# A transformer layer on one core: GpSimd's block arithmetic on VectorE, and a quadrant of W_out read from its own tiles

## The chip, the core and the metric

The kernel runs on one core of a Trainium2 chip. The core has a matrix engine (TensorE, PE in the profile; its weight loads are PEld), a vector engine (VectorE, DVE), an engine for activations, casts and copies (ScalarE, ACT), a general engine (GpSimd, POOL) and SyncE (SP), whose queue issues most of the transfers. Each engine runs its own queue in order and waits for semaphores of the others. The metric is the device time of one execution in microseconds (us), lower is better.

## The reference

One layer of a bidirectional encoder for 1024 tokens of width 1024, all in float32:

```python
h = swiglu(rms_norm(x, g1a), ffn1_w_in, ffn1_w_out)      # (silu(x Wg) * (x Wu)) W_out, d_ff = 2816
x = x + 0.5 * rms_norm(h, g1b)
u = rms_norm(x, gma)
rq, rk, rv, rg, nq, nk, nv, g_ret, g_na = split(u @ w_mix_in)
y_ret = (silu(rg) * headnorm(retention(rotary(rq), rotary(rk), rv))) @ w_ret_out   # 4 heads, both directions
y_na  = neighbourhood_attention_2d(nq, nk, nv, rel_bias) @ w_na_out                # 8 heads, window 8 x 16
x = x + rms_norm((sigmoid(g_ret) * y_ret + sigmoid(g_na) * y_na) @ w_mix_out, gmb)
h = swiglu(rms_norm(x, g2a), ffn2_w_in, ffn2_w_out)
out = x + 0.5 * rms_norm(h, g2b)
```

## The kernel before

**Matmuls in three passes.** Each float32 operand is split in two parts for the matrix engine: `split` (line 56) has ScalarE cast the source to a rounded high half h (line 61), and another engine subtract it from the source to get the low half l (line 62). `mm3` (lines 88 to 90) multiplies high by high, high by low and low by high into one PSUM bank. Weights come by `raw` (a DMA on SP's queue into one of three `wraw` buffers of 128 x 1024), and `piece` splits half of one into tiles `wh` and `wl`, of which there are seven each.

**Winograd products.** The large projections are 2 x 2 block products in seven products in place of eight. `Winograd` (line 234) holds the seven left operands (a11, a12, a22, s1 to s4, each as h and l). `put` makes them from the transposed normed activations for each of eight token tiles: tiles 0 to 3 give a11 and a12, tiles 4 to 7 give a22 and the four sums, with lines 277 and 278 (s3), 283 and 285 (s1, s2), 288 and 289 (s4), and the splits of each. `put` returns the split of s4 as a function that the caller runs later. `Pairs` (line 316) is the loop over pairs of weight tiles: `run` loads two raw tiles g and u, makes the right-hand sums t1 to t4 on DVE (lines 380, 381, 389, 398), splits each and runs seven products of 12 matmuls; the results are added out of PSUM on DVE (lines 387 to 403). `lead` runs the first two products of some pairs ahead; six such pairs stand at the start of the kernel, three of them saved to SBUF by ScalarE.

**The first FFN.** The eight token tiles are normed (`norm_T`: ScalarE squares, GpSimd's `rstd` in line 98, DVE in line 118), transposed by TensorE (line 127) and put. Then `fin.lead` and `ffn_in`: 22 turns of `Pairs.run`, each with a SiLU on ScalarE (line 418) and the product with the up half on DVE (line 420). `LeftFactors` turns each two results into the seven left operands of the output projection: four sums on GpSimd (line 446), then seven splits (ScalarE in line 454, DVE in line 455), one after each product, stored to DRAM by DMAs on GpSimd's queue (line 68).

**ffn_out** multiplies these by W_out, with seven products of 11 k steps and 12 matmuls for each k. The operands g of a step come back from DRAM through `Blocks`, by SP's queue, and the right-hand operand is split by `piece`. The four quadrants of W_out are loaded in three transfers each into `tiles[i][j][n]` (n counts groups of four k). The first product, a11, reads quadrant (0,0): for k below 4 from raw buffers loaded on their own (`b11`), for others from its tiles. The same tiles are loaded whole, since the second product s1 needs t1(k) = (0,1) - (0,0), written over (0,0). `t1` to `t4` (through `sub`, line 559, with a fixed order among themselves) run on GpSimd at set steps. Each product ends with a pass over PSUM on DVE and ScalarE; `ep.square` (line 504) multiplies by the gain on GpSimd, and lines 593 and 594 are two more sums on it. Then norm, residual (line 514) and store.

**Mixing.** Fourteen jobs of `Pairs.run` make the projections; four of them (`fn == "rotary"`) end with `rotate` (lines 886 to 889, four instructions) for each of four parts, parts 0 and 2 on GpSimd and parts 1 and 3 on DVE. Then come neighbourhood attention, retention, gates, and `out_proj`, whose epilogue `Ep` adds the residual in line 229.

**Order.** A scheduler fixes the instructions of each engine at build time from priorities and dependences; the engines then follow that order. A waiting instruction holds up all that stands behind it on its engine.

Of the kernel before, what the change touches and what calls it, by code (L numbers as in the profile page):

```python
# [18 lines left out]
P = 128  # L19
# [19 lines left out]
class Core:  # L39
# [13 lines left out]
        nc.gpsimd.memset(self.mhalf, -0.5)  # L53
        self.small = None

    def split(self, h, l, src, scale=None, eng=None):

        nc = self.nc
        hf = h.bitcast(F32)
        if scale is None:  # L60
            nc.scalar.copy(h, src)  # L61
            (eng or nc.vector).tensor_tensor(l, src, hf, ALU.subtract)  # L62
# [9 lines left out]
        self.nc.sync.dma_start(raw[:, :n], src)  # L72
        return raw

    def piece(self, src, eng=None):
# [3 lines left out]
        self.split(h, l, src, eng=eng)  # L79
        return h, l  # L80

    def load_w(self, src):
# [116 lines left out]
class Ep:  # L199
# [12 lines left out]
    def __call__(self, t, banks):  # L212
        c, nc = self.c, self.c.nc
        y = self.pool.tile([P, D], F32, tag="tmp", name="tmp", bufs=3)
        x = self.pool.tile([P, D], F32, tag="epx", name="epx", bufs=2)
        nc.sync.dma_start(x, self.resid(t))
        ss = c.small.tile([P, 3], F32, tag="ss3", name="ss3", bufs=6)
        f = 4.0 if self.half else 1.0
        for b in range(2):
            nc.scalar.activation(y[:, b * 512:(b + 1) * 512], banks[b], AF.Square,  # L220
                                 scale=(1.0 / 16.0 if self.half else 1.0 / 32.0), accum_out=ss[:, b:b + 1])
        nc.vector.tensor_scalar(ss[:, 2:3], ss[:, 0:1], ss[:, 1:2], f * EPS, ALU.add, ALU.add)
        r = c.rstd(ss[:, 2:3], 1)
        sx = c.small.tile([P, 3], F32, tag="ss3", name="ss3", bufs=6)
        for b in range(2):
            bs = slice(b * 512, (b + 1) * 512)
            nc.vector.scalar_tensor_tensor(y[:, bs], banks[b], r[:, 0:1], self.post[:, bs],
                                           op0=ALU.mult, op1=ALU.mult)
            (nc.gpsimd if t > 5 else nc.vector).tensor_tensor(x[:, bs], y[:, bs], x[:, bs], ALU.add)
            if self.pre is not None:  # L230
                nc.scalar.activation(y[:, bs], x[:, bs], AF.Square, scale=1.0 / 32.0, accum_out=sx[:, b:b + 1])
        (nc.sync.dma_start if self.pre is None else c.store)(self.dst(t), x)
        if self.pre is not None:
            return c.norm_T(x, self.pre, t, self.pool, self.put, sx)


class Winograd:
# [5 lines left out]

    def __init__(self, c, pools, tmp, bufs, spill=None):

        self.c, self.tmp, self.spill, self.s3_on_pool = c, tmp, spill, ()
# [11 lines left out]
    def put(self, t, g, pt):  # L258
        c, nc = self.c, self.c.nc
        ts = slice((t % 4) * P, (t % 4 + 1) * P)  # L260
        if t < 4:
            c.split(*self.part(("a11", "a12")[g], ts), pt)
            return

        def tmp():
            return self.tmp.tile([P, 4, P], F32, tag="cmb", name="cmb", bufs=4)

        h1, l1 = [q.bitcast(F32) for q in self.part("a11", ts)]
        h2, l2 = [q.bitcast(F32) for q in self.part("a12", ts)]

        if g == 0:
            self.a21, self.s3 = tmp(), tmp()
            nc.scalar.copy(self.a21, pt)
            if self.spill is not None:
                c.store(self.spill[:, :, ts], self.a21)
            eng = nc.gpsimd if t in self.s3_on_pool else nc.vector
            eng.tensor_tensor(self.s3, h1, self.a21, ALU.subtract)
            eng.tensor_tensor(self.s3, self.s3, l1, ALU.add)
# [9 lines left out]
        nc.gpsimd.tensor_tensor(s3, h2, s3, ALU.subtract)  # L288
        nc.gpsimd.tensor_tensor(s3, s3, l2, ALU.add)  # L289
        return lambda: c.split(*self.part("s4", ts), s3, eng=nc.gpsimd)  # L290


def xslice(xop):
# [6 lines left out]
class Pairs:  # L300
# [6 lines left out]
        self.last = None  # L307
        self.between = lambda: None

    def product(self, a, b, eng=None):  # L310
        bank = self.c.bank()
        ah, al = self.x.op(a)
        b = self.c.piece(b, eng)
        for k in range(4):
            self.c.mm3(bank, [p[:, k * P:(k + 1) * P] for p in b], (ah[:, k], al[:, k]), k == 0, k == 3)
        self.between()
        return bank
# [12 lines left out]
                               k == 0, k == 3)  # L330
                    yield

    def lead(self, save=None, between=(), on_pool=()):

        n = self.held + self.saved
        for i in (*range(self.held, n), *range(self.held)):
            if i in self.begun:
                continue
            g = self.c.raw(self.srcs[i][0])
            eng = self.c.nc.gpsimd if i in on_pool else None  # L340
            ps = [self.product("a11", g[:, :512], eng), self.product("a12", g[:, 512:], eng)]
            if between:
                f = between.pop(0)()
                if f is not None:
# [81 lines left out]
class LeftFactors:  # L426
# [6 lines left out]
        self.c, self.tmp, self.parts, self.dst, self.later = c, tmp, parts, dst, []  # L433

    def __call__(self, i, gt):
        c, eng, j = self.c, self.c.nc.gpsimd, i // 2
        if i % 2 == 0:
            self.a11, self.a21 = gt[:, 512:], gt[:, :512]
            return
# [44 lines left out]
class Epilogue:  # L484
# [12 lines left out]
            if g is not None:  # L497
                self.c.nc.sync.dma_start(g, src)

    def square(self, t, b, h, junk, out=None, eng=None):  # L500

        c = self.c
        c.nc.scalar.activation(junk, h, AF.Square, scale=1.0 / 16.0, accum_out=self.ss[t][0][:, b:b + 1])
        (eng or c.nc.gpsimd).tensor_tensor(h if out is None else out, h, self.post[:, b * 512:(b + 1) * 512], ALU.mult)

    def steps(self, t, x, halves):
        c, nc = self.c, self.c.nc
# [21 lines left out]
def ffn_out(c, tiles, q, blocks, w_out, gl, ep, side={}):  # L529
# [1 line left out]

    nc = c.nc
    NK = FT // 2
    tt, add = nc.vector.tensor_tensor, nc.gpsimd.tensor_tensor
    spare = [t[2][:, 3] for b in tiles for t in b]
    later, rest, flips, xs = [], [], [], {}

# [18 lines left out]
    order = []  # L556

    def sub(out, a, b):
        e = nc.gpsimd.tensor_tensor(out, a, b, ALU.subtract).ins  # L559
# [28 lines left out]
    def p7(u, b):  # L588
        tt(q[3][:, u], b, q[1][:, u], ALU.add)

        def more():
            xload(u)
            add(q[1][:, u], q[1][:, u], q[2][:, u], ALU.add)
            add(q[2][:, u], q[3][:, u], q[2][:, u], ALU.add)
            ep.square(u, 1, q[2][:, u], spare[u])
        later.extend((more, None))

# [16 lines left out]
    def p3(u, b):  # L614
        e = tt(q[1][:, u], b, q[1][:, u], ALU.add)
        out = q[1][:, u] if ep.pre is not None else q[3][:, u]
        ep.square(4 + u, 1, q[1][:, u], b if ep.pre is not None else spare[2 + u % 2], out, nc.vector if u == 3 else nc.gpsimd)
        g = ep.steps(4 + u, xs[4 + u], (q[0][:, u], out))
        next(g)
        rest.append(g)  # L620
# [7 lines left out]
        if u == 2 and 7 not in xs:  # L628
            xload(7)

    def b11(k):
        if k < 4:
            if k % 2 == 0:
                raws.append(c.raw(w_out[0][:, k * 512:(k + 2) * 512]))
            return raws[-1][:, k % 2 * 512:k % 2 * 512 + 512]
        return quad(k, 0, 0)

    raws = []
    products = (("a11", b11, p1), ("s1", lambda k: quad(k, 0, 0), p5),
                ("s2", lambda k: spare[k % 4], p6), ("s3", lambda k: quad(k, 0, 1), p7),  # L640
                ("a22", lambda k: quad(k, 0, 0), p4), ("a12", lambda k: quad(k, 1, 0), p2),
                ("s4", lambda k: quad(k, 1, 1), p3))
# [15 lines left out]
    def one(u, k, a, b):  # L658
        c.mm3(banks[u], [p[:, u * P:(u + 1) * P] for p in a], b, k == 0, k == NK - 1)

    operand(0)
    for n in (1, 2, 0):
        load(0, 0, n)
    for n, (i, k) in enumerate(steps):
        for m in range(2):
# [46 lines left out]
def na_cores(c, pool, d, bias, fill, n0, n1, n2, side={}):  # L712
# [20 lines left out]
    def load(hp):  # L733
# [4 lines left out]
        for e in range(2):  # L738
            es, es_ = slice(64 * e, 64 * e + 64), slice(64 - 64 * e, 128 - 64 * e)
            for b in range(2):  # L740
                bs = slice(b * 512, b * 512 + 512)
                c.split(kop[hp][e][es, bs], kop[hp][e][es_, bs], kr[es, bs], eng=nc.gpsimd if hp and b else None)

    def vload(hp, cb):
        vr = pool.tile([P, 4, P], F32, tag="vraw", name="vraw", bufs=1)
# [304 lines left out]
def trunk_layer(ctx: ExitStack, tc, x, g1a, w1i, w1o, g1b, gma, wmt, wnv, wrv, logits, dtab, rope, bias,  # L1050
# [36 lines left out]
    with tc.tile_pool(name="norm1", bufs=1) as ep:  # L1087
# [93 lines left out]
    with tc.tile_pool(name="pa", bufs=1) as pa:  # L1181
        evpool[:] = [pa]
        fill.drain()
        turners = (nc.gpsimd, nc.vector, nc.gpsimd, nc.vector)

        def half():
            return pa.tile([P, 512], F32, tag="ev", name="ev", bufs=6)

# [5 lines left out]
        for i, (_, _, f, g, fn) in enumerate(jobs):  # L1194
# [241 lines left out]
```

## Time and profile before

| quantity | value |
|---|---|
| median of 3 runs | 2333.64 us |
| lowest and highest | 2332.41 and 2334.13 us |
| profiled execution, its own time | 2333.33 us |
| its span, first to last instruction | 2331.2 us |
| mean granted TensorE clock | 0.986 |

A page of the profile gives for each engine its busy time and instruction count; the chain that ended last, followed back from the last instruction; and groups of instructions (line, engine, operation, tiles written and read, count, busy time and mean duration of one, and the idle time of the engine in front of them with what ended it). A timeline lists single instructions with start and duration, and in brackets the wait before. A view of stretches gives for each stretch of the span the busy time of each engine with its count of instructions, the granted clock, the DMA share and GB/s.

### The profile page before, as it was taken

How to read it: one execution, taken by the hardware profiler on the slowest of the kernel's cores; microseconds unless marked ns; L12 is line 12 of the kernel's file. 1: busy time of each engine (PE TensorE's matmuls, PEld its weight loads, DVE VectorE, ACT ScalarE, POOL GpSimd, SP SyncE). 2: the span in 40 equal slices, each digit the busy share in tenths (PEclk: the TensorE clock that was granted, in tenths of full speed). 3: DMA queues.
4: the chain of work that ended last, by engine and by line, in shares of the span. 5: the costliest groups of instructions: out<-in, count | busy, mean ns of one | idle time of the engine just before them, and what ended most of it. 6: DMA issues, size and time to landing. Idle time of an engine off the chain costs nothing.

```text
span 2331.2 us, 30432 instructions
## 1 busy us (share of the span) xinstructions
PE 2226.6 (96%) x10288; PEld 1839.9 (79%) x10288; DVE 1672.9 (72%) x2833; ACT 1011.7 (43%) x2102; POOL 789.3 (34%) x889
## 2 busy tenths in 40 slices
PE   6999999989998999999999999999899999998997
PEld 5778888868786887777888888787578888886886
DVE  7888887744458768869875687547998888873443
ACT  6444434322334323248885675226544443432232
POOL 5342424258524134411001222101533242425942
PEclk9999999989999999999999999999899999999999
DMA  4444434498645442357745566766434444539865
GB/s 145 148 150 168 173 126 172 148 405 291 199 156 190 167 167 100 104 178 242 219 155 174 166 219 226 283 211 208 162 132 167 157 161 147 176 115 387 293 229 167
DMA packets 148219, 442.03 MB, mean 190 GB/s; under 512 B 18464, under 2 KB 46240, under 8 KB 145952
## 3 DMA queue, kind: packets, MB, share of 16 engines
q1 hardware_dynamic: 109344, 312.13, 40.6%
q0 software_dynamic: 38720, 127.96, 14.3%
q8 instruction: 82, 1.34, 0.2%
q14 instruction: 73, 0.60, 0.1%
HBM read 303.70 MB, written 140.51 MB: 191 GB/s over the span
## 4 chain that ended last, share of the span: by engine, by line
PE 73%; DVE 11%; issue 6%; POOL 4%; DMA 3%; ACT 2%; SPq 0%; POOLq 0%; DVEq 0%; ACTq 0%
PE ps L88 22%; PE ps L90 22%; PE ps L89 22%; DVE wl L62 2%; DMA wraw<-in_dram 1%; PE pt L90 1%; PE pt L89 1%; PE pt L88 1%; POOL rstd L98 1%; DVE tmp L118 1%; ACT wh L61 1%; POOL cmb L446 1%; DVE t L381 1%; PE ps L765 1%; POOL cmb L289 1%
## 5 line engine op out<-in xcount | busy, mean ns | idle before, releaser
L62 DVE TENSOR_TENSOR wl<-wraw,wh 128x512 fp32r<-128x512 f32 x516 | 383.1, 761 | 80.4 <-ACT wh L61 79.3
L61 ACT CAST wh<-wraw 128x512 fp32r<-128x512 f32 x524 | 306.3, 618 | 225.7 <-DVE wraw L398 69.8
L62 DVE TENSOR_TENSOR wl<-x,wh 128x512 fp32r<-128x512 f32 x146 | 134.4, 930 | 210.9 <-ACT wh L61 210.1
L88 PE MATMUL ps<-wh,g 128*128 128x512 f32 x484 | 190.2, 394 | 22.0 <-DMA g<-g0a 11.5
L61 ACT CAST wh<-x 128x512 fp32r<-128x512 f32 x146 | 89.4, 621 | 232.1 <-PE ps L90 100.1
L89 PE MATMUL ps<-wl,g 128*128 128x512 f32 x484 | 189.9, 392 | 0.0
L90 PE MATMUL ps<-wh,g 128*128 128x512 f32 x484 | 189.8, 392 | 0.0
L559 POOL TENSOR_TENSOR x<-x 128x512 f32<-128x512 f32 x110 | 160.5, 1484 | 52.6 <-DMA x<-in_dram 32.0
L418 ACT ACTIVATE c<-c 128x512 f32<-128x512 f32 x88 | 55.6, 632 | 187.8 <-DVE c L387 95.6
L88 PEld LDWEIGHTS ps<-wh,g 128*128 128x128 f32 x484 | 91.8, 190 | 42.0 <-ACT wh L61 23.1
L61 ACT CAST wh<-t 128x512 fp32r<-128x512 f32 x58 | 36.1, 622 | 177.4 <-DVE t L381 172.7
L90 PE MATMUL ps<-a12h,wl 128*128 128x512 f32 x280 | 109.8, 392 | 3.2 <-DVE wl L62 3.2
L88 PE MATMUL ps<-a11h,wh 128*128 128x512 f32 x280 | 111.5, 398 | 0.7 <-ACT a11h L61 0.7
L90 PE MATMUL ps<-a22h,wl 128*128 128x512 f32 x280 | 109.2, 390 | 1.9 <-DVE wl L62 1.9
L89 PE MATMUL ps<-a11l,wh 128*128 128x512 f32 x280 | 110.5, 395 | 0.0
L88 PE MATMUL ps<-a12h,wh 128*128 128x512 f32 x280 | 110.3, 394 | 0.0
L90 PE MATMUL ps<-a11h,wl 128*128 128x512 f32 x280 | 110.1, 393 | 0.0
L88 PE MATMUL ps<-a22h,wh 128*128 128x512 f32 x280 | 109.7, 392 | 0.0
L89 PE MATMUL ps<-a12l,wh 128*128 128x512 f32 x280 | 109.1, 390 | 0.0
L89 PE MATMUL ps<-a22l,wh 128*128 128x512 f32 x280 | 109.1, 390 | 0.0
L89 PEld LDWEIGHTS ps<-wl,g 128*128 128x128 f32 x484 | 91.9, 190 | 19.6 <-DVE wl L62 0.5
L90 PEld LDWEIGHTS ps<-wh,g 128*128 128x128 f32 x484 | 91.7, 189 | 19.2
(373 smaller groups left out, 6449.4 us busy)
## 6 DMA issues: line engine op xcount, KB each, us to landing
wraw<-in_dram SPq DMA_DIRECT2D x221, 512.0 KB, 4.3
g<-g0s SPq DMA_DIRECT2D x44, 512.0 KB, 4.8
g<-g1s SPq DMA_DIRECT2D x44, 512.0 KB, 4.4
g<-g0a SPq DMA_DIRECT2D x33, 512.0 KB, 3.5
g<-g1a SPq DMA_DIRECT2D x33, 512.0 KB, 4.4
x<-in_dram SPq DMA_DIRECT2D x16, 1024.0 KB, 8.1
g0s<-gth POOLq DMA_DIRECT2D x44, 256.0 KB, 4.0
g0s<-cmb POOLq DMA_DIRECT2D x44, 256.0 KB, 4.1
```

The source lines that it names most:

```text
L61: nc.scalar.copy(h, src)
L62: (eng or nc.vector).tensor_tensor(l, src, hf, ALU.subtract)
L88: mm(ps, a[0], b[0], start=start, stop=False)
L89: mm(ps, a[0], b[1], start=False, stop=False)
L90: mm(ps, a[1], b[0], start=False, stop=stop)
L98: self.nc.gpsimd.tensor_tensor(r[:, :n], ms, self.mhalf[:, :n], ALU.pow)
L118: nc.vector.scalar_tensor_tensor(xn[:, bs], x[:, bs], r[:, 0:1], gain[:, bs], op0=ALU.mult, op1=ALU.mult)
L289: nc.gpsimd.tensor_tensor(s3, s3, l2, ALU.add)
L381: tt(t2, b22, t1, ALU.subtract)
L418: nc.scalar.activation(gate[j], gate[j], AF.Silu)
L446: eng.tensor_tensor(s[o], a, b, op)
L559: e = nc.gpsimd.tensor_tensor(out, a, b, ALU.subtract).ins
```

## The change

All of GpSimd's arithmetic on blocks goes to DVE: the low half of the splits of the lead weights, of `s4` and of some `k` operands, the Winograd sums of lines 277, 278, 288 and 289, the sums of `LeftFactors`, t1 to t4, lines 593 and 594, the gain products of `square`, the rotations of parts 0 and 2, and the residual sums of the last token tiles. GpSimd keeps `rstd`, the setting of constants and the DMAs on its queue. In `ffn_out`, the first product reads quadrant (0,0) from its tiles for every k, the raw loads for it go, and the three loads of that quadrant are issued in the order of n, ahead of the first operand.

```diff
-    def split(self, h, l, src, scale=None, eng=None):
+    def split(self, h, l, src, scale=None):
-            (eng or nc.vector).tensor_tensor(l, src, hf, ALU.subtract)
+            nc.vector.tensor_tensor(l, src, hf, ALU.subtract)
...
-            (nc.gpsimd if t > 5 else nc.vector).tensor_tensor(x[:, bs], y[:, bs], x[:, bs], ALU.add)
+            nc.vector.tensor_tensor(x[:, bs], y[:, bs], x[:, bs], ALU.add)
...
-            eng = nc.gpsimd if t in self.s3_on_pool else nc.vector
-            eng.tensor_tensor(self.s3, h1, self.a21, ALU.subtract)
-            eng.tensor_tensor(self.s3, self.s3, l1, ALU.add)
+            nc.vector.tensor_tensor(self.s3, h1, self.a21, ALU.subtract)
+            nc.vector.tensor_tensor(self.s3, self.s3, l1, ALU.add)
...
-        nc.gpsimd.tensor_tensor(s3, h2, s3, ALU.subtract)
-        nc.gpsimd.tensor_tensor(s3, s3, l2, ALU.add)
-        return lambda: c.split(*self.part("s4", ts), s3, eng=nc.gpsimd)
+        nc.vector.tensor_tensor(s3, h2, s3, ALU.subtract)
+        nc.vector.tensor_tensor(s3, s3, l2, ALU.add)
+        return lambda: c.split(*self.part("s4", ts), s3)
...
-            eng = self.c.nc.gpsimd if i in on_pool else None
-            ps = [self.product("a11", g[:, :512], eng), self.product("a12", g[:, 512:], eng)]
+            ps = [self.product("a11", g[:, :512]), self.product("a12", g[:, 512:])]
...
-        c, eng, j = self.c, self.c.nc.gpsimd, i // 2
+        c, eng, j = self.c, self.c.nc.vector, i // 2
...
-        (eng or c.nc.gpsimd).tensor_tensor(h if out is None else out, h, self.post[:, b * 512:(b + 1) * 512], ALU.mult)
+        c.nc.vector.tensor_tensor(h if out is None else out, h, self.post[:, b * 512:(b + 1) * 512], ALU.mult)
...
-        e = nc.gpsimd.tensor_tensor(out, a, b, ALU.subtract).ins
+        e = tt(out, a, b, ALU.subtract).ins
...
-            add(q[1][:, u], q[1][:, u], q[2][:, u], ALU.add)
-            add(q[2][:, u], q[3][:, u], q[2][:, u], ALU.add)
+            tt(q[1][:, u], q[1][:, u], q[2][:, u], ALU.add)
+            tt(q[2][:, u], q[3][:, u], q[2][:, u], ALU.add)
...
-    def b11(k):
-        if k < 4:
-            if k % 2 == 0:
-                raws.append(c.raw(w_out[0][:, k * 512:(k + 2) * 512]))
-            return raws[-1][:, k % 2 * 512:k % 2 * 512 + 512]
-        return quad(k, 0, 0)
-
-    raws = []
-    products = (("a11", b11, p1), ("s1", lambda k: quad(k, 0, 0), p5),
+    products = (("a11", lambda k: quad(k, 0, 0), p1), ("s1", lambda k: quad(k, 0, 0), p5),
...
-    operand(0)
-    for n in (1, 2, 0):
+    for n in range(3):
         load(0, 0, n)
...
-                c.split(kop[hp][e][es, bs], kop[hp][e][es_, bs], kr[es, bs], eng=nc.gpsimd if hp and b else None)
+                c.split(kop[hp][e][es, bs], kop[hp][e][es_, bs], kr[es, bs])
...
-        fin.lead(lambda: early.tile([P, 512], F32, tag="lead", name="lead", bufs=6), on_pool=(3, 4, 5, 0))
+        fin.lead(lambda: early.tile([P, 512], F32, tag="lead", name="lead", bufs=6))
...
-        turners = (nc.gpsimd, nc.vector, nc.gpsimd, nc.vector)
...
-                    rotate(turners[j], half(), parts[j], *tabs[h])
+                    rotate(nc.vector, half(), parts[j], *tabs[h])
...
-    wx.s3_on_pool = (4, 5)
```

More of the change, by code (lines that the diff above doesn't have):

```diff
@@ L73, in raw, with piece @@
         return raw
-    def piece(self, src, eng=None):
+    def piece(self, src):
         h = self.wpool.tile([P, 512], F32R, tag="wh", name="wh", bufs=7)
         l = self.wpool.tile([P, 512], F32R, tag="wl", name="wl", bufs=7)
-        self.split(h, l, src, eng=eng)
+        self.split(h, l, src)
         return h, l
@@ L244, in __init__ @@
     def __init__(self, c, pools, tmp, bufs, spill=None):
-        self.c, self.tmp, self.spill, self.s3_on_pool = c, tmp, spill, ()
+        self.c, self.tmp, self.spill = c, tmp, spill
         self.pools, self.bufs, self.ops = dict(zip(self.NAMES, (pools[i] for i in (0, 0, 1, 2, 2, 2, 2)))), bufs, {}
@@ L308, in __init__, with product @@
         self.between = lambda: None
-    def product(self, a, b, eng=None):
+    def product(self, a, b):
         bank = self.c.bank()
         ah, al = self.x.op(a)
-        b = self.c.piece(b, eng)
+        b = self.c.piece(b)
         for k in range(4):
@@ L331, in leads, with lead @@
                     yield
-    def lead(self, save=None, between=(), on_pool=()):
+    def lead(self, save=None, between=()):
         n = self.held + self.saved
@@ L498, in gains, with square @@
                 self.c.nc.sync.dma_start(g, src)
-    def square(self, t, b, h, junk, out=None, eng=None):
+    def square(self, t, b, h, junk, out=None):
         c = self.c
         c.nc.scalar.activation(junk, h, AF.Square, scale=1.0 / 16.0, accum_out=self.ss[t][0][:, b:b + 1])
-        (eng or c.nc.gpsimd).tensor_tensor(h if out is None else out, h, self.post[:, b * 512:(b + 1) * 512], ALU.mult)
+        c.nc.vector.tensor_tensor(h if out is None else out, h, self.post[:, b * 512:(b + 1) * 512], ALU.mult)
     def steps(self, t, x, halves):
@@ L533, in ffn_out @@
     NK = FT // 2
-    tt, add = nc.vector.tensor_tensor, nc.gpsimd.tensor_tensor
+    tt = nc.vector.tensor_tensor
     spare = [t[2][:, 3] for b in tiles for t in b]
@@ L616, in p3 @@
         out = q[1][:, u] if ep.pre is not None else q[3][:, u]
-        ep.square(4 + u, 1, q[1][:, u], b if ep.pre is not None else spare[2 + u % 2], out, nc.vector if u == 3 else nc.gpsimd)
+        ep.square(4 + u, 1, q[1][:, u], b if ep.pre is not None else spare[2 + u % 2], out)
         g = ep.steps(4 + u, xs[4 + u], (q[0][:, u], out))
```

## The prediction, made before the result

> **What bounds the kernel now.** I read the page's header, busy times and chain first.
>
> ```profile
> span 2331.2 us, 30432 instructions
> PE 2226.6 (96%) x10288; PEld 1839.9 (79%) x10288; DVE 1672.9 (72%) x2833; ACT 1011.7 (43%) x2102; POOL 789.3 (34%) x889
> PE 73%; DVE 11%; issue 6%; POOL 4%; DMA 3%; ACT 2%; SPq 0%; POOLq 0%; DVEq 0%; ACTq 0%
> ```
>
> The profiled run took 2333.33 us, so 2.1 us lie outside its span; the runs' median is 2333.64 us, and no correction is made. TensorE is the bound: it lacks 104.6 us of the span, and no matmul is added or removed. So the question is only in which of those few idle places the change adds or removes time. An average load of 72% on DVE says nothing about that; the places do. I went on to the groups of GpSimd (columns: line, engine, operation, tiles, shapes, count, busy us, mean ns, idle before).
>
> ```profile
> L559 POOL TENSOR_TENSOR x<-x 128x512 f32<-128x512 f32 x110 | 160.5, 1484 | 52.6 <-DMA x<-in_dram 32.0 <-DVE wl L62 18.9
> L446 POOL TENSOR_TENSOR cmb<-gt 128x512 f32<-128x512 f32 x44 | 61.4, 1412 | 4.2 <-DVE gt L420 4.0
> L446 POOL TENSOR_TENSOR cmb<-gt,cmb 128x512 f32<-128x512 f32 x44 | 58.6, 1331 | 0.8
> ...
> L504 POOL TENSOR_TENSOR q<-q,gain 128x512 f32<-128x512 f32 x30 | 42.9, 1445 | 102.5 <-ACT ps L503 83.3 <-DVE q L615 17.4 <-ACT x L503 1.7
> ...
> L288 POOL TENSOR_TENSOR cmb<-a12h,cmb 128x512 f32<-128x512 f32 x12 | 19.2, 1603 | 27.4 <-DVE s2l L62 27.4
> L289 POOL TENSOR_TENSOR cmb<-cmb,a12l 128x512 f32<-128x512 f32 x12 | 18.5, 1542 | 0.9
> ...
> L62 POOL TENSOR_TENSOR s4l<-cmb,s4h 128x512 fp32r<-128x512 f32 x12 | 17.0, 1420 | 8.1 <-ACT s4h L61 8.0
> L888 POOL TENSOR_TENSOR ev<-ev,tab 128x512 f32<-128x512 f32 x8 | 13.1, 1632 | 0.6
> L889 POOL TENSOR_TENSOR ev<-ev 128x512 f32<-128x512 f32 x8 | 13.0, 1622 | 0.6
> L886 POOL TENSOR_TENSOR ev<-ev,tab 64x512 f32<-64x512 f32 x8 | 11.8, 1472 | 24.6 <-DVE ev L387 21.8 <-DVE ev L403 2.7
> L887 POOL TENSOR_TENSOR ev<-ev,tab 64x512 f32<-64x512 f32 x8 | 11.7, 1462 | 0.5
> L62 POOL TENSOR_TENSOR wl<-wraw,wh 128x512 fp32r<-128x512 f32 x8 | 11.4, 1432 | 0.2
> ```
>
> These twelve groups are 304 instructions and 439 us, and all of them move to DVE. A few smaller groups go with them (L593, L594, the k splits, L229, L277, L278): by the code 30 instructions, taken at the same price.
>
> **What one moved instruction costs.** Two timelines, DVE's and then GpSimd's, at the same time (start, duration, engine, line):
>
> ```profile
> 844.30 0.68 DVE L380 TENSOR_TENSOR wraw<-wraw 128x512 f32<-128x512 f32 x1
> 845.01 1.66 DVE L381 TENSOR_TENSOR t<-wraw 128x512 f32<-128x512 f32 x1
> ```
>
> ```profile
> 844.50 1.63 POOL L888 TENSOR_TENSOR ev<-ev,tab 128x512 f32<-128x512 f32 x1
> ```
>
> A DVE instruction that starts alone takes 0.68 us, one beside a GpSimd instruction 1.66. Back to back, DVE instructions start 0.60 to 0.61 us apart (the 0.60 row of the chain below). So 334 more cost DVE 334 x 0.61 = 204 us. What DVE gets back is the stretch, about 1.0 us where it meets one. The two largest groups of DVE show how often that is:
>
> ```profile
> L62 DVE TENSOR_TENSOR wl<-wraw,wh 128x512 fp32r<-128x512 f32 x516 | 383.1, 761 | 80.4 <-ACT wh L61 79.3
> L62 DVE TENSOR_TENSOR wl<-x,wh 128x512 fp32r<-128x512 f32 x146 | 134.4, 930 | 210.9 <-ACT wh L61 210.1
> ```
>
> Against 0.68 they are (0.761 - 0.68) x 516 + (0.930 - 0.68) x 146 = 78 us too long. They are 31% of DVE's busy time (517 of 1672.9); if the rest is stretched alike, up to twice as much again, I bound the whole between 78 and 240 us and take 140. DVE then goes from 1673 to about 1740 us (1637 to 1799): nearly unchanged on average, while GpSimd empties. Whether time is lost is decided by the order on one queue instead of two.
>
> The Trainium skill, "SBUF — State Buffer", section "Who interferes with whom", states that a DVE instruction with two SBUF inputs and a GpSimd instruction that reads SBUF exclude each other for a whole instruction. The pair of timelines agrees (DVE at 845.01 ends just after GpSimd at 846.13). By it up to 334 us would come back, which the two largest groups bear out in part only; rival 1 below, worked out from rows, is what it would do here.
>
> **Start, before the first full pair of weights (0 to 160 us).** Before, GpSimd makes the eight lead splits while DVE is on norms and operands. After, the built order puts the second lead pair's low half (wl) on DVE behind 75 rows: all the norms and nearly all Winograd operands.
>
> ```profile
> 11.81 4.63 POOL wl L62 x3
> ...
> 28.64 0.66 DVE tmp L118
> 29.43 0.60 DVE cmb L278
> ```
>
> Those are the chain's pieces; below, TensorE on the product banks alone (stretch, length, busy and count), then all engines (PE, PEld, DVE, ACT, POOL busy, clock, DMA).
>
> ```profile
> 0.00:60.00 60.00, 28.78 (x110) 1.00 0.40 140
> 60.00:70.00 10.00, 8.96 (x38) 1.00 0.34 105
> ```
>
> ```profile
> 100.00:160.00 60.00, 54.56 (x229) 43.43 (x229) 53.18 (x82) 24.49 (x43) 23.66 (x34) 0.97 0.53 189
> ```
>
> The 75 rows are by the built order 51 two-tensor instructions (x 0.61), 16 of L118 (x 0.66) and 8 tiny ones (0.2): 43.3 us from about 7.7, with some 3 us of waits for norms: 54 us (50 without waits, 57 with twice as many). TensorE has until then 24 matmuls of the first pair and 12 beginnings; 108 are left to the 144th, at 0.223 us a start (194.43 us for 872 in the row 494 to 690 below) 24.1 us: 78.1. After such a hole it starts slowly: the rows at 478 to 480 below have four starts in 1.84 us, 0.46 each; by an estimate of 4 us at that pace, 2 us more: 80.1. The records before count 110 by 60 us and 148 by 70, so the 144th stands near 69. The delay is 11.1 us. From 100 to 160 before loses 5.4 us of idle and 3% of clock, 1.8 us, with DVE and GpSimd behind; I take 4.5 of these 7.2 back, because L446 on GpSimd no longer stretches DVE's instructions, and not all, because DVE is late itself. Start: **+6.6** (-2 with 50 us, no slow clock and all 7.2 back; +14 with 57 and none back).
>
> **The two starts of ffn_out.** Before, k = 0 of the first product comes from raw buffers split in advance and runs at once; then TensorE waits for g of k = 1. DVE's timeline there, and TensorE's at the end of the wait:
>
> ```profile
> 476.93 1.89 DVE L62 TENSOR_TENSOR wl<-x,wh 128x512 fp32r<-128x512 f32 x3
> ```
>
> ```profile
> 478.29 0.77 PE L88 MATMUL ps<-wh,g 128*128 128x512 f32 x1 [11.55 <-DMA g<-g0a]
> ...
> 480.13 0.63 PE L89 MATMUL ps<-wl,g 128*128 128x512 f32 x1
> ```
>
> After, k = 0 needs W_out's first tile, and its split stands on DVE among the last L455 splits. DVE splits k = 1 to 3 only at 476.93, so k = 0's split comes by 477 or, without the stretch (1.89 against 0.68 and its like), some us earlier. Its 12 matmuls (12 x 0.223 = 2.7 us, or 12 x 0.46 = 5.5 at the slow pace) move into a hole of 11.55 us, which covers them if the split is ready by 473; at 477 some 8 fall behind 478.3, 3.7 us at 0.46. By the code two raw loads of 512 KB go, so g may land a little earlier. I take **+1** each, +2 for both (-2 to +3.7 each).
>
> The page "TensorE: Matmul & The Clock Gate" of the Trainium skill, section "What's actually happening", has TensorE at half clock after about 3.4 us of idling, for as long again. The rows at 478 to 480 agree. It speaks against the move: before, k = 0 runs ahead of the hole at full pace. By it k = 0 would cost about 5.4 us inside the hole, an estimate, where the rows above say 5.5.
>
> **ffn_in, ffn_out in their run, mixing, norms, tail.**
>
> ```profile
> DVE gt L455 <- POOL cmb L446: 51.7, 24, 4.8
> ```
>
> ```profile
> 494.00:690.00 196.00, 194.43 (x872) 160.23 (x870) 94.06 (x118) 63.53 (x126) 112.25 (x83) 1.00 0.71 254
> 845.00:980.00 135.00, 130.84 (x568) 105.42 (x567) 117.52 (x148) 36.65 (x65) 57.71 (x55) 1.00 0.32 113
> 700.00:760.00 60.00, 49.83 (x216) 39.93 (x217) 53.89 (x77) 28.87 (x57) 27.05 (x26) 0.94 0.55 181
> ```
>
> ```profile
> PE ps L90 <- DVE wl L62: 3.3, 8, 0.5
> ```
>
> In ffn_in 51.7 us of DVE waits for L446 vanish, but nearly all of them lie beside a busy TensorE; 88 x 0.61 = 54 us take their place. At the ramp of the second FFN a little comes back: **-1** (-3 to +3). In ffn_out's run (494 to 690) DVE is 48% busy; some 80 moved instructions x 0.61 = 49 us, less the stretch, leave it below 75%, so the 110 L559 stay covered: **0** (to +3, if the dense part with four DVE instructions per 2.7 us falls behind).
>
> The last row is the window 845 to 1000 (rotary jobs): eight waits of TensorE for wl, 3.3 us, in a place where GpSimd stretches wl. They go. But 16 rotary instructions now stand in one queue ahead of the next wl, 9.8 us where a product lasts 2.7, with the seven wl buffers as cover: if it runs dry once per rotary job, 1.1 us each for four jobs. Net **+1** (-3.3 to +9). In the norm and operand stages (700 to 760, and the like before the second FFN) DVE is 90% busy already, GpSimd half; the moved sums are 12 and 20 x 0.61 = 7 and 12 us, and the stretch given back is about as much: **-2** together (-6 to +6). The 30 gain products (L504) are half hidden; at the tail L504 no longer stretches its neighbour: **-0.5**. The k splits have waits on both sides: 0.
>
> Sum: 6.6 + 2 - 1 + 0 + 1 - 2 - 0.5 = **+6.1**, so 2333.3 + 6.1 = 2339.4 us. Its own range, with start and mixing half-way to their bounds, is 2334 to 2347.
>
> **The rivals.** (1) *Faster: contention was the price.* All stretch comes back and one queue at 0.61 serves better than two at 1.7. Start +1, ffn_in -3, mixing -3.3, norms -5, starts of ffn_out -2, tail -0.5: -12.8, or 2320.5. For it: DVE's load hardly rises, and stretched instructions stand on the chain. Against: at the start GpSimd's work is a pure second queue, and its absence is in the order.
> (2) *Slower: the rotary chains stall TensorE.* DVE serves products in order, so 4 x 0.61 = 2.4 us of each of 8 moved rotations meet TensorE: 19.5 us in place of 1 from the point at which the wl buffers run dry: 2339.4 + 18.5 = 2358. For it: DVE is 87% busy in that window and TensorE already waits for wl. Against: its 148 instructions there at 0.61 would be 90 us, where 117.5 are shown; the rest is stretch and goes.
> (3) *Slower: W_out comes late.* k = 0 starts after g has landed, 5.5 us at each start: 11 instead of 2, or 2348. It decides if DVE reaches the split after 478.
> (4) *Nothing shows*: DVE's slack takes all, the order at the start costs what the ramp returns: 2333.
>
> **How the numbers follow.** The forecast 0.38, of which 0.10 ends within 0.2% (4.7 us, about what a measurement of this kernel can tell from no change) and 0.28 above; rival 1 0.26, all faster; rival 2 0.16 and rival 3 0.10, slower; rival 4 0.10, same. So faster 0.26, same 0.20, slower 0.54. The range reaches from 2321, which leaves out rival 1's outer half (0.13), to 2358, which leaves out half of rival 2 (0.08).
>
> **What would show it.** After: DVE near 1740 us with subtractions at 0.68 everywhere and GpSimd below 320; at the start TensorE with a hole until about 54 us, ended by wl; in ffn_out's first product a wait for wl or g ending within 3 us of 478; in 845 to 1000 no 0.4-us waits, but one or two longer ones for wl at each rotary job. Wrong if the start's hole ends before 45 us, if DVE's busy time falls below 1640, or if waits for wl above 3 us stand in the rotary jobs.

## The result and the profile after

| | before | after |
|---|---|---|
| median of 14 runs each | 2335.69 us (2331.66 to 2337.85) | 2340.22 us (2334.41 to 2343.44) |
| ratio of after to before, 95% interval | | 1.0021 [1.0013, 1.0028] |
| profiled execution: span | 2331.2 us | 2336.8 us |

The change costs about 0.2%, 4.5 us between the medians; 2339.4 us was forecast, 6.1 us above the profile of before. In the changed kernel most line numbers are lower (L455 of before is L453 there, L987 is L976). The page after begins so, with the two largest groups of splits:

```profile
span 2336.8 us, 30365 instructions
PE 2228.1 (95%) x10288; PEld 1843.3 (79%) x10288; DVE 1720.8 (74%) x3167; ACT 1013.3 (43%) x2102; POOL 316.9 (14%) x555
...
L62 DVE TENSOR_TENSOR wl<-wraw,wh 128x512 fp32r<-128x512 f32 x516 | 345.0, 684 | 98.2 <-ACT wh L61 97.5
...
L62 DVE TENSOR_TENSOR wl<-x,wh 128x512 fp32r<-128x512 f32 x154 | 104.5, 688 | 152.5 <-ACT wh L61 152.5
```

DVE has 334 instructions more, and only 47.9 us more of busy time: its subtractions fell from 761 and 930 ns to 684 and 688. Of 204 us put on it, 156 came back as vanished stretch: by the two traces, the instructions that DVE had before are together 155 us shorter. DVE's busy time alone therefore gives no reason for a loss. To find the place, the same product is looked up in both timelines. Here is the last matmul of the first s4 product, the end of the first turn of `ffn_in`; first before, then after (start, duration):

```profile
82.58 0.39 PE L90 MATMUL ps<-s4h,wl 128*128 128x512 f32 x1
```

```profile
92.92 0.39 PE L90 MATMUL ps<-s4h,wl 128*128 128x512 f32 x1
```

After is 10.3 us late there. Following such marks through the timelines gives a lag for each stage (us, after minus before, from the two profiled executions; "own" is what the stage itself adds):

| mark | before | after | lag | own |
|---|---|---|---|---|
| end of the first s4 product | 82.97 | 93.31 | +10.3 | +10.3 |
| end of the 6th s4 product | 159.33 | 168.02 | +8.7 | -1.7 |
| end of the first `ffn_in` | 464.02 | 472.66 | +8.6 | 0.0 |
| first transpose in the epilogue of `ffn_out` | 637.09 | 645.71 | +8.6 | 0.0 |
| end of the first s4 product of mixing | 764.77 | 771.65 | +6.9 | -1.7 |
| end of the last one | 1030.67 | 1037.05 | +6.4 | -0.5 |
| 41st transpose of yn in retention | 1397.49 | 1402.10 | +4.6 | -1.8 |
| 64th, the last | 1464.61 | 1474.31 | +9.7 | +5.1 |
| first transpose before the second FFN | 1591.75 | 1600.58 | +8.8 | -0.9 |
| end of the first s4 product of the second FFN | 1710.73 | 1717.28 | +6.6 | -2.3 |
| end of the second `ffn_in` | 2096.88 | 2103.49 | +6.6 | 0.0 |
| end of the span | 2331.2 | 2336.8 | +5.6 | -1.0 |

The whole loss and more is made in the first 93 us, and one other place, 5.1 us in retention, is taken up below. How far the smaller steps repeat is seen in the profiles of the experiments, and is said in the part on the prediction. TensorE's waits in the first 160 us, before and then after (who waited for whom: us in total, times, longest):

```profile
PE pt L127 <- DVE tmp L118: 14.2, 6, 8.5
PE ps L90 <- DVE wl L62: 4.3, 3, 1.9
```

```profile
PE pt L127 <- DVE tmp L118: 17.4, 5, 8.5
PE ps L90 <- DVE wl L62: 10.0, 4, 7.2
```

DVE's timeline after shows what TensorE waits for, and TensorE's shows the end of the wait:

```profile
51.79 0.68 DVE L62 TENSOR_TENSOR s1l<-cmb,s1h 128x512 fp32r<-128x512 f32 x1
52.39 0.68 DVE L62 TENSOR_TENSOR wl<-wraw,wh 128x512 fp32r<-128x512 f32 x1
52.99 0.68 DVE L62 TENSOR_TENSOR s2l<-cmb,s2h 128x512 fp32r<-128x512 f32 x1
```

```profile
53.13 0.80 PE L90 MATMUL ps<-a11h,wl 128*128 128x512 f32 x1 [7.24 <-DVE wl L62]
```

The second lead pair's wl stands between the s1 and s2 splits of the last operand tile. It could have been made 40 us earlier, since ScalarE had cast its high half here:

```profile
12.21 0.62 ACT L61 CAST wh<-wraw 128x512 fp32r<-128x512 f32 x1
```

By stretches (length, busy time of PE, PEld, DVE, ACT and POOL, clock, DMA) the same place after reads:

```profile
20.00:40.00 20.00, 13.74 (x61) 10.12 (x60) 18.55 (x33) 13.17 (x29) 2.78 (x4) 0.91 0.21 72
40.00:60.00 20.00, 9.40 (x32) 7.00 (x31) 19.79 (x33) 8.82 (x16) 0.00 (x0) 0.57 0.16 53
60.00:80.00 20.00, 20.00 (x89) 16.54 (x89) 7.26 (x11) 8.07 (x13) 0.00 (x0) 1.00 0.42 132
```

From 40 to 60 us DVE is full while TensorE is busy for less than half of the time (9.40 of 20 us), and then DVE is a third busy while TensorE catches up on leads: the two work one after the other.

### The profile page after: what moved, and what is told of

It is laid out like the page before. It is cut to its first block, busy times and chain, and to the rows that moved or that the text cites. A ratio compares the mean times of both kernels' runs of the same rounds, so it can differ in the third digit from the quotient of the medians.

```text
span 2336.8 us, 30365 instructions
## 1 busy us (share of the span) xinstructions
PE 2228.1 (95%) x10288; PEld 1843.3 (79%) x10288; DVE 1720.8 (74%) x3167; ACT 1013.3 (43%) x2102; POOL 316.9 (14%) x555
## 4 chain that ended last, share of the span: by engine, by line
PE 62%; issue 20%; DVE 8%; POOL 4%; DMA 3%; ACT 2%; POOLq 0%; DVEq 0%; SPq 0%; ACTq 0%
PE ps L90 19%; PE ps L89 19%; PE ps L88 19%; PE pt L89 1%; PE pt L90 1%; PE pt L88 1%; DVE wl L62 1%; DMA wraw<-in_dram 1%; PE ps L754 1%; PE pt L773 1%; POOL rstd L98 1%; DVE tmp L118 1%; ACT wh L61 0%; POOL g1s L68 0%; POOL rg L68 0%
## 5 line engine op out<-in xcount | busy, mean ns | idle before, releaser
L62 DVE TENSOR_TENSOR wl<-wraw,wh 128x512 fp32r<-128x512 f32 x516 | 345.0, 684 | 98.2 <-ACT wh L61 97.5
L61 ACT CAST wh<-wraw 128x512 fp32r<-128x512 f32 x516 | 301.5, 619 | 231.3 <-PE ps L89 79.9
L62 DVE TENSOR_TENSOR wl<-x,wh 128x512 fp32r<-128x512 f32 x154 | 104.5, 688 | 152.5 <-ACT wh L61 152.5
L61 ACT CAST wh<-x 128x512 fp32r<-128x512 f32 x154 | 94.5, 621 | 250.8 <-PE ps L90 128.0
L88 PE MATMUL ps<-wh,g 128*128 128x512 f32 x484 | 189.7, 395 | 12.4 <-ACT wh L61 12.4
L98 POOL TENSOR_TENSOR rstd<-ss,mhalf 128x1 f32<-128x1 f32 x80 | 55.4, 694 | 582.3 <-DVE ss L507 385.9
```

The costliest lines, as they stand in the source:

```text
L62: nc.vector.tensor_tensor(l, src, hf, ALU.subtract)
L88: mm(ps, a[0], b[0], start=start, stop=False)
L98: self.nc.gpsimd.tensor_tensor(r[:, :n], ms, self.mhalf[:, :n], ALU.pow)
```

## The experiments

All ratios are to the kernel before on the same chip, with their 95% intervals.

### Lead splits back on GpSimd

The argument `eng` is passed on through `product`, `piece` and `split` as in the kernel before; those lines are left out here.

```diff
-            ps = [self.product("a11", g[:, :512]), self.product("a12", g[:, 512:])]
+            eng = self.c.nc.gpsimd if i in on_pool else None
+            ps = [self.product("a11", g[:, :512], eng), self.product("a12", g[:, 512:], eng)]
...
-        fin.lead(lambda: early.tile([P, 512], F32, tag="lead", name="lead", bufs=6))
+        fin.lead(lambda: early.tile([P, 512], F32, tag="lead", name="lead", bufs=6), on_pool=(3, 4, 5, 0))
```

> The changed kernel with one part undone: the low halves of lead pairs 3, 4, 5 and 0 (eight splits) are again made by GpSimd. Theory (the start is the whole loss, and it is the lead splits' place behind the operands on DVE): TensorE runs the lead pairs while DVE is on the operands, the first s4 product ends near 83 to 86 us instead of 93.3, and the time falls by 7 to 9 us, to below the kernel before by 2 to 5 us (ratio 0.998 to 0.999). Rival (the s4 sums on DVE are what makes the operands late, and the leads only fill the wait): the operands are complete as late as before, the s4 product ends within 2 us of 93.3, and the ratio stays at 1.001 to 1.002.

Measured 2327.81 us, ratio 0.9973 [0.9963, 0.9982]; the first s4 product ends at 82.7. Eight instructions of 334 turn the sign: the theory holds, and the gain is larger than it said (a ratio of 0.998 to 0.999).

### The whole start back on GpSimd

```diff
+        eng = nc.gpsimd if self.s4_on_pool else nc.vector
-        nc.vector.tensor_tensor(s3, h2, s3, ALU.subtract)
-        nc.vector.tensor_tensor(s3, s3, l2, ALU.add)
-        return lambda: c.split(*self.part("s4", ts), s3)
+        eng.tensor_tensor(s3, h2, s3, ALU.subtract)
+        eng.tensor_tensor(s3, s3, l2, ALU.add)
+        return lambda: c.split(*self.part("s4", ts), s3, eng=eng)
```

with the leads as in the run above, and `s4_on_pool` set for the first FFN alone.

> The changed kernel with the whole start undone: lead splits and the sums and splits of s4 of the first FFN again on GpSimd, all else as changed. Theory (lead splits alone): like the run with the leads alone, within 2 us. Rival (both needed, or the s4 sums alone): 3 us or more faster than the run with the leads alone.

Measured 2329.42 us, ratio 0.9970 [0.9957, 0.9983], the first s4 product at 83.0. So moving the s4 sums of the start back as well gives nothing that these runs can tell.

### The raw buffers for W_out back

```diff
+    def b11(k):
+        if k < 4:
+            if k % 2 == 0:
+                raws.append(c.raw(w_out[0][:, k * 512:(k + 2) * 512]))
+            return raws[-1][:, k % 2 * 512:k % 2 * 512 + 512]
+        return quad(k, 0, 0)
...
-    for n in range(3):
+    operand(0)
+    for n in (1, 2, 0):
         load(0, 0, n)
```

> The changed kernel with the reading of the first quadrant of W_out undone (raw buffers for k below 4, the old order of loads). Theory (the matmuls of k = 0 lie inside a wait for g that is there anyway): within 2 us of the changed kernel, ratio to before 1.001 to 1.003, with k = 0 run at once and a wait of 10 to 12 us for g at each of the two places. Rival (the later k = 0 costs its 5.5 us at each place and the gain of emptied contention hides it): 6 us or more faster than the changed kernel, ratio below 1.000.

Measured 2341.8 us, ratio 1.0026 [1.0013, 1.0038], 1.6 us above the changed kernel: the theory's interval, and no sign of the rival. The waits for g are there again, 12.4 and 12.1 us long. Its start is 2.1 us later than the changed kernel's in the profile (the first s4 product ends at 95.4), though DVE's first 110 instructions are the same in the same order, so a difference this small says nothing of W_out.

The same edit on the kernel with the leads on GpSimd, where the start doesn't disturb:

> The run with the leads on GpSimd, and in addition the raw buffers for W_out as before: against that run it shows W_out's part alone, without the loss at the start. Theory (k = 0 lies in a wait that is there anyway): within 2 us of the run with the leads alone, ratio 0.997 to 0.998. Rival a (k = 0 inside the hole costs 5 us at each place): ratio 0.995 or less. Rival b (reading from the tiles gains, by fewer bytes ahead of g): ratio 0.9985 or above.

Measured 2327.28 us, ratio 0.9963 [0.9950, 0.9977], 0.5 us from the run with the leads alone (the ratio, taken against other runs of before, is lower than the theory had it, and not as low as rival a): W_out's part is worth nothing that these runs can tell. The waits of TensorE between 463 and 490 show why. Before:

```profile
PE ps L88 <- DMA g<-g0a: 11.5, 1, 11.5
```

After:

```profile
PE ps L88 <- ACT wh L61: 6.4, 1, 6.4
PE ps L89 <- DVE wl L62: 4.3, 1, 4.3
```

and DVE's and TensorE's rows there, after:

```profile
483.41 1.29 DVE L453 TENSOR_TENSOR cmb<-cmb,gth 128x512 fp32r<-128x512 f32 x2 [3.62 <-ACT gth L452]
484.62 4.29 DVE L62 TENSOR_TENSOR wl<-x,wh 128x512 fp32r<-128x512 f32 x7
```

```profile
479.01 2.08 PE L88 MATMUL ps<-wh,g 128*128 128x512 f32 x4 [6.35 <-ACT wh L61]
485.36 0.79 PE L89 MATMUL ps<-wl,g 128*128 128x512 f32 x1 [4.27 <-DVE wl L62]
```

One hole of 11.5 us became two of 10.7 together, with four matmuls of k = 0 between them and eight behind. The wl of k = 0 does stand behind the last L453 splits (L455 before), as foreseen: DVE sits idle for 3.62 us in front of them, waiting for ScalarE's gth.

### The lead splits on DVE, alone

```diff
-        fin.lead(lambda: early.tile([P, 512], F32, tag="lead", name="lead", bufs=6), on_pool=(3, 4, 5, 0))
+        fin.lead(lambda: early.tile([P, 512], F32, tag="lead", name="lead", bufs=6))
```

> The kernel before with one part of the change alone: the eight lead splits on DVE, all else as before. Theory: the loss at the start appears alone, first s4 product near 91 to 94 us instead of 83.0 and the time 6 to 9 us above the kernel before (ratio 1.0026 to 1.004). Rival (the loss needs all parts together, DVE being full only with the s4 sums too): ratio 1.000 to 1.001.

Measured 2343.42 us, ratio 1.0037 [1.0025, 1.0049], the first s4 product at 95.2. The ratio is in the theory's interval, and the product is 1.2 us later than it said. By the ratio this one edit of the kernel before costs more than the whole change (1.0021); the rest of the change gives some back.

### All on DVE, the lead splits put first

```diff
-        b = self.c.piece(b)
+        if first:
+            with self.c.tc.high_priority(offset=first):
+                b = self.c.piece(b)
+        else:
+            b = self.c.piece(b)
...
-        fin.lead(lambda: early.tile([P, 512], F32, tag="lead", name="lead", bufs=6))
+        fin.lead(lambda: early.tile([P, 512], F32, tag="lead", name="lead", bufs=6), first=400)
```

> The changed kernel, all arithmetic on DVE as changed, but the splits of the lead pairs get a higher priority at build time: the second pair's low halves stand in DVE's order behind 9 and 10 instructions instead of 74 and 76. Theory (it is the place of the splits in DVE's one queue, not DVE's load): the first s4 product ends at 83 to 87 us instead of 93.3, the time is within 3 us of the run with the leads on GpSimd (ratio 0.997 to 0.999). Rival (load: the eight splits cost DVE 5 us that GpSimd would have done beside it, and all operands come later by as much): the s4 product ends at 88 us or later, ratio 0.9995 or above.

Measured 2326.2 us, ratio 0.9956 [0.9943, 0.9968]; the first s4 product ends at 77.3, 16 us earlier than in the changed kernel and 5.7 earlier than before: more than the theory gave (83 to 87 us, 0.997 to 0.999). Not an instruction moved to another engine. Its stretch from 40 to 60 us:

```profile
40.00:60.00 20.00, 20.00 (x97) 16.42 (x96) 19.86 (x34) 11.35 (x21) 0.00 (x0) 1.00 0.12 42
```

DVE is as full as in the changed kernel (19.86 against 19.79 us), but TensorE is full beside it (20.00 against 9.40). It is the place in the queue, and the load rival falls. The priority goes to all twelve splits of the six lead pairs, though, and so also to the four that the kernel before has on DVE: there they start between 54.75 and 62.07 us, here between 34.55 and 42.87. What these four add to the gain was not separated; it is an obvious candidate for the start's being better than before and not only as good.

The same priority on the kernel before, with all else left on GpSimd:

> The kernel before, all else on GpSimd as it was, but the lead splits on DVE and put first there. Theory (place decides, so the start is as good as with GpSimd's help, and the rest of the change is worth a few us of its own): first s4 product at 77 to 84 us, ratio 0.997 to 1.000, 3 to 7 us behind the run with all on DVE and the splits put first. Rival (the rest of the change is worth nothing): within 1.5 us of that run, ratio 0.9950 to 0.9965.

Measured 2332.47 us, ratio 0.9986 [0.9977, 0.9995], the first s4 product at 81.7, 6.3 us behind the run above. So the other 326 moves and W_out together gain about 0.3%; by the profiles 4.4 of the 6.3 us are there at the end of the first s4 product (81.7 against 77.3).

### t1 to t4 back on GpSimd

```diff
-        e = tt(out, a, b, ALU.subtract).ins
+        e = nc.gpsimd.tensor_tensor(out, a, b, ALU.subtract).ins
```

on the kernel with the leads on GpSimd.

> The run with the leads on GpSimd, and in addition t1 to t4 (110 instructions) on GpSimd again. Theory (they are covered by TensorE's products on either engine): wl splits stretched again, DVE's busy time nearly the same, time within 1.5 us of the run with the leads alone, ratio 0.9968 to 0.998. Rival (their move off GpSimd is where the gain of the other places came from): 3 us or more slower, ratio 0.9985 or above.

Measured 2325.8 us, ratio 0.9958 [0.9945, 0.9970], 2.0 us faster than the run with the leads alone, and so beyond what the theory gave, on the other side from the rival. The intervals of the two runs overlap; that the gain does not come from t1 to t4 is shown, that their move costs something is not. The stretch comes back, as expected:

```profile
L62 DVE TENSOR_TENSOR wl<-x,wh 128x512 fp32r<-128x512 f32 x154 | 137.7, 905 | 194.0 <-ACT wh L61 193.5
```

These are the splits of `ffn_out`, beside which t1 to t4 run: 905 ns each here, 689 in the run with the leads alone and 930 before. So the stretch of this group is due to t1 to t4 on GpSimd, and the kernel does not get slower by it.

### Both, the lead splits first and t1 to t4 on GpSimd

> The run with the lead splits put first on DVE, and in addition t1 to t4 on GpSimd: the parts that were best each by themselves. Theory (the two places do not touch each other; t1 to t4 on GpSimd gave 0 to 2 us): ratio 0.994 to 0.9960, at or below the run with the splits put first. Rival (the 2 us of the run with t1 to t4 on GpSimd were the scatter of its few runs): ratio 0.9953 to 0.9968.

Measured 2323.95 us, ratio 0.9948 [0.9936, 0.9961]: the fastest version. It stands 2.2 us under the run with the splits put first, again inside the intervals, and its ratio lies in the part that only the theory gave, by a little.

### The later Winograd sums back on GpSimd

The s4 edit above, set for mixing and the second FFN in place of the first, on the kernel with the leads on GpSimd, together with

```diff
-            nc.vector.tensor_tensor(self.s3, h1, self.a21, ALU.subtract)
-            nc.vector.tensor_tensor(self.s3, self.s3, l1, ALU.add)
+            eng = nc.gpsimd if t in self.s3_on_pool else nc.vector
+            eng.tensor_tensor(self.s3, h1, self.a21, ALU.subtract)
+            eng.tensor_tensor(self.s3, self.s3, l1, ALU.add)
```

> The run with the leads on GpSimd, and in addition the Winograd sums of the two later operand stages (s4 in both, s3 of two token tiles before the second FFN) on GpSimd again. Theory (there the queue on two engines with contention is slower than DVE alone, and the stages give back 1.5 and 2.3 us in the changed kernel): 2 to 5 us slower than the run with the leads alone, ratio 0.998 to 0.9995. Rival (the gain in these stages comes from other moved work, such as the gain products and the residual sums): within 1 us of it, ratio 0.9968 to 0.9978.

Measured 2332.25 us, ratio 0.9988 [0.9979, 0.9997]: 4.4 us slower than with the leads alone, as the theory had it. By the marks, the stretch from the first transpose before the second FFN to the first s4 product takes 117.4 us with these sums on DVE and 121.5 with them on GpSimd; from the first transpose of the normed tokens before mixing to its first s4 product the two are alike (101.6 and 101.3). TensorE's waits from 1590 to 1725, first with the sums on DVE, then on GpSimd:

```profile
PE ps L90 <- DVE gl L62: 0.3, 1, 0.3
```

```profile
PE ps L90 <- DVE gl L62: 4.3, 4, 2.1
```

With the sums on GpSimd, TensorE waits 4.0 us longer for the low halves gl, which DVE makes; its other waits in this window grow and shrink by up to 2.1 us and together change by less than 1.

### The rotations back on GpSimd

```diff
-                    rotate(nc.vector, half(), parts[j], *tabs[h])
+                    rotate((nc.gpsimd, nc.vector)[j % 2], half(), parts[j], *tabs[h])
```

on the kernel with the leads on GpSimd.

> The run with the leads on GpSimd, and in addition the rotations of parts 0 and 2 on GpSimd again. Theory (in the rotary jobs the eight small waits and the four longer ones are worth the same): within 1.5 us of the run with the leads alone, ratio 0.9965 to 0.998, waits for wl from 845 to 1000 of about 0.4 us each again. Rival (DVE alone serves the rotations at a loss that shows as longer waits): 2 us or more faster, ratio below 0.9965 and waits for wl in that stretch below 2 us.

Measured 2326.67 us, ratio 0.9959 [0.9946, 0.9973], 1.1 us from the run with the leads alone (beside which the kernel before was 1.3 us faster). The ratio is in the range that the rival gave, but its waits are not, and the stretch itself is unmoved: from the first to the last s4 product of mixing it is 266.0 us here and 266.2 there. The waits from 845 to 1010, first with the rotations on DVE in the run with the leads alone, then on both engines here:

```profile
PE ps L90 <- DVE wl L62: 4.9, 4, 1.8
```

```profile
PE ps L90 <- DVE wl L62: 3.4, 8, 0.6
```

Four waits of 1.2 us on average against eight of 0.4: the kind changes as predicted, and the sum by 1.5 us, of which the length of the stretch shows 0.2. In the changed kernel the four waits are 4.0 us together, the longest 1.1.

### The changed kernel once more

> The changed kernel once more, for a second profile of it. In its first profile 5.1 us were lost in retention behind one transfer of rg that landed late. Theory (a late transfer of that execution, no part of the change): the stretch between the 41st and the 64th transpose of yn is back within 1 us of the 67.1 us of before. Rival (the new order of the instructions brings it about each time): again above 71 us.

Ratio 1.0021 [1.0011, 1.0031]. The stretch in retention takes 67.2 us, 67.1 before and 72.2 in the first profile. The wait in the first profile was this, in DVE's timeline:

```profile
1422.27 0.42 DVE L976 TENSOR_TENSOR rg<-pt,rg 128x256 f32<-128x256 f32 x1 [4.49 <-DMA rg<-rg]
```

It is an event of that execution: the changed kernel's second profile is without it, and the run with the splits put first, whose marks show 72.1 us there, has it again. What makes this transfer late in two of them was not tried. The second profile is not shorter for it (2339.3 us): in mixing it loses 2.2 us against before, where the first gained 0.5, with one wait for wl of 2.2 us, and from the second `ffn_in`'s end to the last matmul it takes 1.3 us more than the first.

## Why the prediction was right, and where it wasn't

**The start** was the right mechanism. The hole was to end at 54 us by wl, and ended at 53.13 by wl. The 144th matmul was to be 11.1 us late; it starts at 79.32 in place of 68.62, 10.7 late, and the first s4 product is 10.3 us late. The slow pace after the hole lasts from 53.13 to 56.7, 3.6 us at 0.43 a start, where 4 us at 0.46 were estimated. Too large was the part that comes back: 4.5 us were taken of the 7.2 that before loses from 100 to 160, and 1.7 us came. Nor is the reason given for it, L446 off GpSimd, shown: from the first to the 6th s4 product it is 76.4 us before and 74.7 after, but also 74.8 with the lead splits alone on DVE and all of L446 on GpSimd. The term was +6.6 and measured +8.6. (The rows of the prediction without waits end at 43.3 + 7.7 = 51 us, not at 50; only the lower bound of this term hangs on it.) That it is the place of the splits and not DVE's load, the prediction had said ("decided by the order on one queue"); the run with the splits put first shows it.

**W_out** was +1 at each place. Counted from the last s4 product of `ffn_in`, the 13th matmul of `ffn_out`, the first of k = 1, starts 14.26 us later before and 16.27 after: 2.0 us late, since eight matmuls of k = 0 do stand behind the hole. But the slow pace is paid only once, before by k = 1 and after by k = 0, and at the 25th matmul the difference is 0.65 us (19.11 and 19.76), at the second place 0.24 (17.94 and 18.18); in the second profile of the changed kernel 0.6 and 1.6. So the step was right, with the scatter as large as the term. Later in the first `ffn_out` the 0.65 is made up, where a wait of 1.5 us at its end becomes one of 0.8, which is why the table shows 0.0. The 5.5 us for twelve matmuls at the slow pace were too many: behind the hole of before twelve take 4.84 us (478.29 to 483.13), since the last ones are at full pace again. The split, forecast by 477 in the time of before, came at 484.62, less the lag of 8.64 this is 476.0; so rival 3's condition, after 478, was not met.

**ffn_in and t1 to t4** were put at -1 and 0. The second FFN's ramp gave nothing, the first's is counted in the start. The run with t1 to t4 back on GpSimd shows them covered on either engine, within 2 us.

**Mixing** was +1 and measured -0.5 in the first profile and +2.2 in the second: longer waits for wl at each rotary job, as said, but rival 2's 19.5 us are far off. Over all profiles the stretch from the first to the last s4 product of mixing takes 265.9 to 266.0 us with half of the rotations on GpSimd (four profiles) and 265.4 to 268.1 with all on DVE (ten), so the term lies inside the scatter.

**The operand stages** were put at -2 and gave 1.7 + 2.3 = 4.0 us. This is the largest gain. The second of them repeats: it takes 119.0 to 121.5 us in the four profiles that have these sums on GpSimd, and 115.9 to 117.4 in the ten that have them on DVE; the run with the sums alone back on GpSimd (121.5) shows that they are its cause. The first takes 127.0 to 130.4 in the first four and 125.1 to 127.3 in the others, so that its 1.7 us are less sure. Whether the gain comes by the stretch of DVE's splits or by GpSimd's own slower pace was not separated. The tail, from the last matmul to the end of the span, was put at -0.5 and gave 1.2 (12.2 us before, 11.0 after).

**Neighbourhood attention and what lies around it** was put at 0, and the two profiles differ by 1.8 us up to the 41st transpose of yn. That is not shown to be a gain: the two runs that have the instructions of before here (the lead splits on DVE alone, and the kernel before with them put first) take 365.5 and 363.9 us for it, where before takes 366.8 and the changed kernel 365.0 in its first profile and 366.1 in its second.

So the mechanism of the start was right, and that the sum came so close is in part luck, since errors cancel: the start was 2 us too small, the gains of the operand stages 2 too small, and the late transfer in retention, 5.1 us of the profiled execution, stood in no step. The second profile, without that transfer, is 8 us above the profile of before, and the medians differ by 4.5. That the forecast time lies within 1 us of the median is luck too: it started from 2333.3 us, where the 14 runs of before have a median of 2335.69. Rival 1 was half right: without the start's loss the rest of the change gains 0.27%. What it missed is the one thing that the prediction held against it, the order at the start.

## What to carry to other kernels

When work goes from two queues to one, the sum of busy times says little: here DVE took 334 instructions more for 48 us more. Read where the built order puts the few instructions that the bound engine waits for next; eight lead splits, six of them behind 74 or more other instructions, cost 12 us between the medians, and a priority for all twelve lead splits gave 14. Try the order before the engine: all on DVE with those splits put first is 0.44% faster than the kernel before.

## What the runs showed that was not expected

One moved instruction costs DVE far less than its own time: 47.9 us for 334 is 0.14 us each, where an instruction takes 0.61. And the same order of instructions does not give the same start each time: the changed kernel and the one with raw buffers for W_out both have a hole of 7.2 us, but in the latter it ends at 54.59 in place of 53.13, the slow pace behind it lasts 5.3 us in place of 3.6, and the first s4 product ends at 95.4 in place of 93.3. A difference of 2 us at the start needs more than one profile.
